# One layer of a hybrid decoder on one core: weight buffers of one width in two tiles, and weight sums made one step before their split

## The chip, the cores and the metric

The kernel runs on one core of a Trainium2 chip. Its engines work side by side, each through its own queue in order: PE (TensorE) multiplies matrices, DVE (VectorE) does elementwise arithmetic, ACT (ScalarE) copies and applies functions, POOL (GpSimd) and SP (SyncE) issue DMAs. The metric is the device time of one execution in microseconds (us). Before the change it was 2711.05 us, the median of 3 runs (2710.53 to 2716.68).

## The reference, cut to what matters

One layer with 512 positions and a model width of 2048, all in float32:

```python
mod = (silu(c) @ w_ada + b_ada)          # shifts, scales, gates
h = rms_norm(x, g_attn) * (1.0 + sc_a) + sh_a
x = x + gt_a * parallel_mixers(h, ...)   # sparse attention and latent attention, gated, then w_o
h = rms_norm(x, g_ffn) * (1.0 + sc_f) + sh_f
x = x + gt_f * conv_ffn(h, w_up, w_conv, b_conv, w_down)

def conv_ffn(h, w_up, w_conv, b_conv, w_down):
    u = h @ w_up                          # 512 x 2048 @ 2048 x 11264
    up = jnp.pad(u, ((0, 0), (CONV_W - 1, 0), (0, 0)))
    conv = b_conv
    for j in range(CONV_W):               # 3 taps over the positions, causal
        conv = conv + w_conv[j] * up[:, j:j + S]
    gate, val = jnp.split(conv, 2, axis=-1)
    return (jax.nn.silu(gate) * val) @ w_down   # 512 x 5632 @ 5632 x 2048
```

The change concerns the products with `w_up` and `w_down` and part of the mixers' gate projection.

## The kernel before

**Precision.** PE multiplies in a format narrower than float32. So every operand is split into a high part (a copy by ACT) and a low part (the rest, by DVE); helper `split`, lines 129 to 131. Each product is then three matmuls: high x high, high x low, low x high.

**Seven products.** Three loops use `seven` (line 935): a part of the gate projection (8 pairs), the up projection (40 of its 44 pairs), and the down projection (4 chunks of 5, 6, 6 and 5 row blocks, 8 pairs each). A "pair" is two column blocks of 128 of the weight. Its product, split into 2 x 2 blocks, is made with seven block products instead of eight. The weight comes as four blocks, `L[11]`, `L[21]`, `L[22]`, `L[12]`, each 128 partitions by K x 128 columns (1024 in the up projection, 640 or 768 in the down projection). The seven products need these blocks and sums of them: s3 = L21 - L11, then L21 + L22, that less L11, and L12 less the latter. DVE makes the sums, in place but for s3 (`comb`, line 979). The activations' sums are made beforehand.

**Steps.** A pair has seven steps, in the order p1, p7, p6, p2, p5, p4, p3. The function of that name (lines 995 to 1033) loads, sums and splits a step's weight; `prepare` (line 1065) calls it AHEAD steps before PE's matmuls of that step (2, and 3 in the down projection). A step has 3 K matmuls of 256 columns: 24 in the up projection, 15 or 18 in the down projection. After them `e1` to `e3` take the bank (a PSUM accumulator) out: a copy by ACT (lines 985 and 987) or a sum on DVE (lines 991 and 993), which I call bank sum. Two steps later, or one on another bank between, PE accumulates on the same bank again and must wait for that. After a pair's last step `ffn_out` convolves the two results (ACT line 1379, DVE lines 1380 and 1381), multiplies them and stores them as `f`; the down projection ends in a multiplication by the gate and a sum into `x1_d` or the output.

**Buffers.** Weights lie in raw buffers (`rawq`, a queue: a load takes the oldest, `done` puts one back at the end) and in buffers for the split (`hi_b`, `lo_b`, used in turn by the counter `cnt["wt"]`). `weight_bufs` makes them in a pool of their own: 5 raw of 1104 columns and 3 pairs for the split, and from the down projection on 7 raw of 768 and 4 pairs, for which the pool is closed and opened anew in the same memory (`turn`, line 1572, after the matmuls of the up projection's last step). There are also 81 slots of 512 columns for everything else (`get`, `put`); a slot that was put back rests for a few steps. In the first 34 of the 40 up pairs (`slots=True`) s3 and L12 don't lie in raw buffers but in two slots each; loads, sums and splits of them are then made in two pieces.

**Order.** Dependencies follow the stretches of a tile that instructions read and write. A planner orders each engine's instructions: it plays the program with its own estimates of durations and puts an instruction in its engine's queue when it believes that engine and data are ready, program order breaking ties. Weight loads go through SP's queue (line 968), which stands at a load until its buffer is free. POOL's queue stores and reloads f tiles (lines 1397, 1406 and 1482); `ahead` (line 1496) loads and splits these for the down projection as slots come free, from the last 56 steps of the up projection on.

## Time and profile before

| | us |
|---|---|
| median of 3 runs | 2711.05 |
| profiled execution | 2708.11 |
| its span, first to last instruction | 2706.3 |
| seven products of the gates, from the first matmul to the last | 614.5 to 784.7 |
| of the up projection, 34 pairs with slots | 1402.7 to 2100.7 |
| of the up projection, 6 pairs in raw buffers | 2100.7 to 2221.2 |
| of the down projection | 2227.1 to 2701.9 |

The profile is of one execution. Busy time is the time in which an engine ran an instruction; idle time before a group of instructions is put down to what ended it, the releaser. "DVE slot L981 <- DMA raw<-in_w_ups" reads: DVE, about to run line 981 with a slot as result, waited for a DMA from the up weights into a raw buffer. Where a column of numbers follows it, it is the total in us, the number of times and the longest. A line is often that of a helper: L130 and L131 are the high and the low part of every split, L981 every weight sum, L1082 to L1084 the matmuls of every step of seven products. DMA-issuing instructions stand on SPq, the sequencer of SP.

### The profile page before, as it was taken

The page shows a single profiled execution, that of the slowest core. Times are in us where ns is not written, and L with a number is a line of the kernel's source. Part 1 is how long each engine was busy: PE and PEld are TensorE (multiplying, and loading weights), DVE is VectorE, ACT ScalarE, POOL GpSimd, SP SyncE. Part 2 cuts the span into 40 slices and gives each one's busy share as a digit, 9 for nine tenths or more (in the row PEclk, how much of TensorE's full clock was granted, in tenths as well). Part 3 has the DMA queues.
Part 4 walks back from the last instruction along what each step waited for, and adds up shares of the span by engine and source line. Part 5 has one row for each costly group of instructions (what it writes and reads, how often), then busy time and mean ns, then how long its engine had stood idle before and what let it go on. Part 6 is the DMA issues. An engine that isn't in the chain of part 4 may idle for free.

```text
span 2706.3 us, 45437 instructions
## 1 busy us (share of the span) xinstructions
PE 2613.8 (97%) x17200; PEld 2345.9 (87%) x17200; DVE 2180.2 (81%) x3669; ACT 1281.9 (47%) x2069; POOL 363.6 (13%) x663
## 2 busy tenths in 40 slices
PE   6999999999999999999999999999999999999999
PEld 5787687778997767788789999999999988899999
DVE  7977976688878667983778888888889888778777
ACT  4333434334444455322545555555555555545454
POOL 1001011110032222110100000000001032413120
PEclk8999899999999999999999999999999999999999
DMA  9953136665585588962333343334334456767563
GB/s 340 339 160 98 33 112 213 196 217 164 195 265 158 164 260 283 332 231 94 133 128 114 124 139 115 127 114 141 127 110 148 131 178 181 188 163 192 138 204 116
DMA packets 220559, 464.33 MB, mean 172 GB/s; under 512 B 24330, under 2 KB 65700, under 8 KB 220340
## 3 DMA queue, kind: packets, MB, share of 16 engines
q1 hardware_dynamic: 175156, 344.93, 39.0%
q0 software_dynamic: 45152, 116.50, 15.0%
q8 instruction: 134, 2.20, 0.3%
q14 instruction: 85, 0.70, 0.1%
q10 hardware_dynamic: 32, 0.01, 0.0%
HBM read 397.11 MB, written 64.23 MB: 170 GB/s over the span
## 4 chain that ended last, share of the span: by engine, by line
PE 53%; DVE 16%; issue 15%; DMA 13%; POOL 2%; ACT 1%; SPq 0%; DVEq 0%; POOLq 0%; ACTq 0%
PE bank L134 9%; PE bank L135 9%; PE bank L136 9%; PE bank L1082 7%; PE bank L1083 7%; PE bank L1084 7%; DVE wlo L131 6%; DMA raw<-in_w_ups 5%; DMA slot<-in_w_ada 2%; DMA raw<-in_w_down 2%; DVE raw L981 2%; DVE slot L981 1%; DVE slot L1380 1%; DMA raw<-in_w_in 1%; DVE slot L1381 1%
## 5 line engine op out<-in xcount | busy, mean ns | idle before, releaser
L1082 PE MATMUL bank<-slot,whi 128*128 128x256 f32 x3920 | 1108.2, 283 | 44.8 <-DVE slot L991 13.1
L1083 PE MATMUL bank<-slot,whi 128*128 128x256 f32 x3920 | 1101.6, 282 | 0.4 <-DVE slot L131 0.4
L1084 PE MATMUL bank<-slot,wlo 128*128 128x256 f32 x3920 | 1094.3, 282 | 5.7 <-DVE wlo L131 5.6
L1082 PEld LDWEIGHTS bank<-slot,whi 128*128 128x128 f32 x3920 | 743.2, 190 | 58.3 <-DVE slot L993 16.5
L1084 PEld LDWEIGHTS bank<-slot,wlo 128*128 128x128 f32 x3920 | 737.2, 189 | 8.6 <-DVE wlo L131 8.3
L1083 PEld LDWEIGHTS bank<-slot,whi 128*128 128x128 f32 x3920 | 742.2, 189 | 0.9 <-DVE slot L131 0.6
L130 ACT ACTIVATE whi<-raw 128x1024 fp32r<-128x1024 f32 (+2 forms) x458 | 424.6, 928 | 463.8 <-PE bank L1083 352.0
L131 DVE TENSOR_TENSOR wlo<-raw,whi 128x1024 fp32r<-128x1024 f32 (+2 forms) x458 | 482.1, 1058 | 54.3 <-ACT whi L130 53.0
L122 ACT ACTIVATE whi<-raw 128x1024 fp32r<-128x1024 f32 (+4 forms) x182 | 187.2, 1031 | 392.0 <-PE bank L136 198.9
L123 DVE TENSOR_TENSOR wlo<-raw,whi 128x1024 fp32r<-128x1024 f32 (+4 forms) x182 | 216.5, 1191 | 147.7 <-ACT whi L122 146.3
L981 DVE TENSOR_TENSOR raw<-raw,raw 128x1024 f32<-128x1024 f32 (+2 forms) x252 | 265.2, 1053 | 68.7 <-DMA raw<-in_w_down 47.5
L135 PE MATMUL bank<-wlo,slot 128*128 128x512 f32 (+2 forms) x768 | 297.0, 387 | 0.9 <-DVE wlo L123 0.9
L134 PE MATMUL bank<-whi,slot 128*128 128x512 f32 (+2 forms) x768 | 289.6, 390 | 6.8 <-ACT slot L401 4.3
L136 PE MATMUL bank<-whi,slot 128*128 128x512 f32 (+2 forms) x768 | 292.0, 384 | 0.0
L135 PE MATMUL bank<-slot,whi 128*128 128x512 f32 (+1 forms) x656 | 263.0, 401 | 1.2 <-DVE slot L703 1.1
L134 PE MATMUL bank<-slot,whi 128*128 128x512 f32 (+1 forms) x656 | 260.8, 403 | 3.1 <-ACT slot L1370 2.3
L136 PE MATMUL bank<-slot,wlo 128*128 128x512 f32 (+1 forms) x656 | 257.5, 401 | 0.4 <-DVE wlo L123 0.4
L134 PEld LDWEIGHTS bank<-whi,slot 128*128 128x128 f32 x768 | 145.8, 190 | 38.1 <-ACT slot L401 4.4
L135 PEld LDWEIGHTS bank<-wlo,slot 128*128 128x128 f32 x768 | 146.2, 190 | 29.4 <-DVE wlo L123 1.4
L739 DVE SCALAR_TENSOR_TENSOR slot<-slot,c_act,slot 128x512 f32<-128x512 f32 x203 | 149.6, 749 | 25.3 <-DMA slot<-in_w_ada 24.3
L136 PEld LDWEIGHTS bank<-whi,slot 128*128 128x128 f32 x768 | 144.7, 189 | 28.4 <-issue 0.3
L130 ACT ACTIVATE whi<-slot 128x512 fp32r<-128x512 f32 x204 | 128.0, 628 | 82.0 <-PE bank L1083 60.7
(294 smaller groups left out, 3115.0 us busy)
## 6 DMA issues: line engine op xcount, KB each, us to landing
slot<-in_w_ada SPq DMA_DIRECT2D x344, 256.0 KB, 5.6
raw<-in_w_ups SPq DMA_DIRECT2D x126, 512.0 KB, 4.3
raw<-in_w_in SPq DMA_DIRECT2D x50, 512.0 KB, 3.6
raw<-in_w_down SPq DMA_DIRECT2D x64, 384.0 KB, 5.1
raw<-in_w_down SPq DMA_DIRECT2D x64, 320.0 KB, 4.2
slot<-f POOLq DMA_DIRECT2D x154, 128.0 KB, 3.8
slot<-in_w_ups SPq DMA_DIRECT2D x68, 256.0 KB, 2.7
f<-slot POOLq DMA_DIRECT2D x66, 256.0 KB, 5.3
```

What stands on the lines that cost most here:

```text
L122: A.activation(hi, raw[:, :w], AF.Copy)
L123: V.tensor_tensor(lo, raw[:, :w], r32(hi), ALU.subtract)
L130: A.activation(dst_hi, src, AF.Copy)
L131: V.tensor_tensor(dst_lo, src, r32(dst_hi), ALU.subtract)
L134: PE.matmul(o, lh, rh, start=first, stop=False)
L135: PE.matmul(o, lh, rl, start=False, stop=False)
L136: PE.matmul(o, ll, rh, start=False, stop=last)
L739: V.scalar_tensor_tensor(acc, ts[i], c_act[:, k:k + 1], acc, op0=ALU.mult, op1=ALU.add)
L981: V.tensor_tensor(part(o, x, y), part(a, x, y), part(b, x, y), op)
L1082: PE.matmul(o, wh[:, ks], rh, start=first and k == 0, stop=False, skip_group_check=True)
L1083: PE.matmul(o, wh[:, ks], rl, start=False, stop=False, skip_group_check=True)
L1084: PE.matmul(o, wl[:, ks], rh, start=False, stop=last, skip_group_check=True)
```

## The change

Five things are changed together.

1. All pairs of the up projection use raw buffers for s3 and L12, none uses slots; all loads, sums and splits are of one piece.
2. The raw buffers are stretches of one tile, `raw`, and those for the split stretches of another, `whl`; both exist for the whole program. `weight_bufs` lays them out anew without closing a pool. New raw buffers are put in the queue in the order in which the old ones at their place were put back.
3. A step has two functions: one that loads and sums (a1, a7, a6, a4), called one step before the other, which splits (p1 to p3). So s3, both sums of p6 and the sum into L12 (out of p5, into a4) are made one step before their split in program order. s3 takes the buffer that was put back last (`rawq.pop()`).
4. `turn` is called at every step of the up projection. At its last step but one it lays out the buffers anew, and at its last two steps it prepares the down projection's first two; a third is prepared after the loop.
5. The counter of the split buffers is set before the up projection so that its last three steps use them in the order 0, 1, 2.

```diff
-    wpool = ExitStack()
-    hi_b, lo_b, rawq = [], [], deque()
+    WR, WS = 5 * 1104, 6 * 1104
+    wraw = pool.tile([P, WR], F32, name="raw")
+    whl = pool.tile([P, WS], F32R, name="whl")
+    hi_b, lo_b, rawq, raw_at = [], [], deque(), []
+    cnt = {"wt": 0, "half": 0, "at": 0}
     def weight_bufs(nr, nh, w):
-        wpool.close()
-        wp = wpool.enter_context(tc.tile_pool(name=f"w{w}", bufs=1))
+        assert nr * w <= WR and 2 * nh * w <= WS and len(rawq) == len(raw_at)
+        age = [[i for i, t in enumerate(rawq) if t is b[0]][0] for b in raw_at]
+        def freed(x):
+            return max([a for a, (_, lo, hi) in zip(age, raw_at) if lo < x + w and x < hi], default=0)
+        raw_at[:] = [(wraw[:, i * w:(i + 1) * w], i * w, (i + 1) * w) for i in sorted(range(nr), key=lambda i: freed(i * w))]
         rawq.clear()
-        rawq.extend([wp.tile([P, w], F32, name=f"raw{w}_{i}") for i in range(nr)])
-        hi_b[:] = [wp.tile([P, w], F32R, name=f"whi{w}_{i}") for i in range(nh)]
-        lo_b[:] = [wp.tile([P, w], F32R, name=f"wlo{w}_{i}") for i in range(nh)]
+        rawq.extend(b[0] for b in raw_at)
+        hi_b[:] = [whl[:, 2 * i * w:(2 * i + 1) * w] for i in range(nh)]
+        lo_b[:] = [whl[:, (2 * i + 1) * w:(2 * i + 2) * w] for i in range(nh)]
+        cnt["wt"] = 0
...
-            def new(slots=False):
-                if slots:
-                    return [(get(), 0, T), (get(), T, W)]
-                return [(rawq.popleft(), 0, W)]
...
-            def load(blk, slots=False):
-                t = new(slots)
-                for b, x, y in t:
-                    SP.dma_start(b[:, :y - x], p.load(blk)[:, x:y])
+            def load(blk):
+                t = rawq.popleft()
+                SP.dma_start(t[:, :W], p.load(blk))
                 return t
...
             def comb(o, a, b, op):
-                for x, y in cuts(o, a, b):
-                    V.tensor_tensor(part(o, x, y), part(a, x, y), part(b, x, y), op)
+                V.tensor_tensor(o[:, :W], a[:, :W], b[:, :W], op)
...
-            def p1():
+            def a1():
                 L[11] = load(0)
                 L[21] = load(1)
+            def p1():
                 return hilo(L[11])
+            def a7():
+                L["s3"] = rawq.pop()
+                comb(L["s3"], L[21], L[11], ALU.subtract)
+                L[22] = load(3)
             def p7():
-                s3 = new(p.slots)
-                comb(s3, L[21], L[11], ALU.subtract)
-                r = hilo(s3)
-                done(s3)
-                L[22] = load(3)
+                r = hilo(L["s3"])
+                done(L["s3"])
                 return r
-            def p6():
+            def a6():
                 comb(L[21], L[21], L[22], ALU.add)
                 comb(L[11], L[21], L[11], ALU.subtract)
-                r = hilo(L[11])
-                L[12] = load(2, p.slots)
-                return r
+                L[12] = load(2)
+            def p6():
+                return hilo(L[11])
...
             def p5():
                 r = hilo(L[21])
+                done(L[21])
+                return r
+            def a4():
                 comb(L[12], L[12], L[11], ALU.subtract)
                 done(L[11])
-                done(L[21])
-                return r
...
+            return (((a1, p1), X, r11, e1, True), ((a7, p7), Y, t3, e7, True), ((a6, p6), X, t2, e6, False),
+                    ((none, p2), Z, r21, e2, False), ((none, p5), X, t1, e5, False),
+                    ((a4, p4), Y, t4, e4, False), ((none, p3), X, r22, e3, False))
         def prepare(q):
+            for i in range(0 if q == 0 else q + 1, min(q + 2, len(steps))):
+                steps[i][0][0]()
             if q < len(steps):
-                ready[q] = steps[q][0]()
-        def start():
-            for q in range(AHEAD):
+                ready[q] = steps[q][0][1]()
+        def start(*qs):
+            for q in qs or range(AHEAD):
                 prepare(q)
         def run(then=None):
             for q, (_, o, r, ev, first, K) in enumerate(steps):
                 prepare(q + AHEAD)
+                if then:
+                    then(q - len(steps))
...
-                if then and q == len(steps) - 1:
-                    then()
...
-    work = [Pair(rs, lambda blk, i=i: w_ups[i, blk], ffn_out(i), slots=i < NF_ - 10) for i in range(NF_ - 4)]
+    work_up = [Pair(rs, lambda blk, i=i: w_ups[i, blk], ffn_out(i)) for i in range(NF_ - 4)]
...
-    def turn():
-        weight_bufs(7, 4, 768)
-        down_start()
+    def turn(q):
+        if q == -2:
+            assert cnt["wt"] % 3 == 0
+            weight_bufs(7, 4, 768)
+        if q >= -2:
+            down_start(q + 2)
+    cnt["wt"] = 3 - len(work_up) * 7 % 3
     up_start()
     up_run(turn)
+    down_start(2)
     down_run()
```

26 lines of the change are left out of this document (7 added, 19 removed).

## The prediction

> **What bounds the kernel now.** I read the page first, then PE's waits, then a table of stages, then the instructions in order of time. In the first part of the page PE is busy for 97% of the span; the count of splits at L122 and the landing time of a weight load, below it, are used further down.
>
> ```profile
> span 2706.3 us, 45437 instructions
> ...
> PE 2613.8 (97%) x17200; PEld 2345.9 (87%) x17200; DVE 2180.2 (81%) x3669; ACT 1281.9 (47%) x2069; POOL 363.6 (13%) x663
> ...
> L122 ACT ACTIVATE whi<-raw 128x1024 fp32r<-128x1024 f32 (+4 forms) x182 | 187.2, 1031 | 392.0 <-PE bank L136 198.9
> ...
> raw<-in_w_ups SPq DMA_DIRECT2D x126, 512.0 KB, 4.3
> ```
>
> PE's waits (engine, line, releaser: us, times, longest) name DVE's bank sums (L993 in the up projection, L991 in the down projection):
>
> ```profile
> PE bank L1082 <- DVE slot L991: 13.1, 9, 3.1
> PE bank L1082 <- DVE slot L993: 11.2, 24, 1.2
> ```
>
> The table of stages (us; busy time of PE, PEld, DVE, ACT and POOL with their instructions; granted clock; DMA share; GB/s): the 34 pairs of the up projection with slots, its 6 pairs in wide buffers, the idle time at the turn, the first pair of the down projection, and its chunks of row blocks.
>
> ```profile
> 1402.70:2100.70 698.00, 683.17 (x5713) 676.43 (x5712) 619.79 (x893) 372.34 (x578) 44.66 (x83) 1.00 0.38 127
> 2100.70:2221.20 120.50, 119.59 (x1011) 119.14 (x1009) 108.71 (x137) 68.48 (x97) 25.04 (x47) 1.00 0.47 147
> 2221.20:2227.10 5.90, 0.28 (x4) 0.07 (x2) 2.82 (x5) 1.99 (x4) 2.64 (x5) 0.76 0.84 264
> 2227.10:2245.90 18.80, 15.86 (x106) 14.54 (x107) 18.71 (x31) 12.15 (x21) 6.39 (x12) 0.89 0.72 234
> 2245.90:2345.40 99.50, 91.61 (x737) 89.52 (x736) 79.49 (x120) 56.30 (x97) 33.09 (x52) 0.98 0.70 184
> 2345.40:2473.80 128.40, 122.89 (x1010) 120.56 (x1009) 100.91 (x133) 68.99 (x110) 35.24 (x56) 1.00 0.67 172
> 2473.80:2601.90 128.10, 121.84 (x1010) 120.29 (x1009) 98.84 (x133) 64.86 (x104) 32.41 (x49) 1.00 0.66 175
> 2601.90:2702.00 100.10, 100.10 (x842) 99.75 (x840) 81.86 (x122) 50.71 (x85) 9.56 (x17) 1.00 0.44 138
> ```
>
> Time divided by matmuls gives each stage's pace. A pair has 7 x 24 = 168 matmuls, so the first row has 34 x 168 = 5712 (122.2 ns each), the second 1008 (119.5 ns). The last chunk, where PE is never idle, takes 100.1 / 840 = 119.2 ns. At these paces the up projection has 698.0 - 5712 x 0.1195 = 15 us to give. The down projection has 99.5 - 735 x 0.1192 = 11.9, then 128.4 - 1008 x 0.1192 = 8.2 and 7.9: together 28. The turn, with its first pair of 105 matmuls, has 5.9 + 18.8 - 12.5 = 12.2. So 55 us is about all that this change can reach.
>
> What makes the bank sums late are DVE's own waits (same columns):
>
> ```profile
> DVE slot L981 <- DMA raw<-in_w_ups: 57.3, 29, 4.2
> DVE raw L981 <- DMA raw<-in_w_down: 47.5, 26, 3.9
> ```
>
> L981 is a weight sum. The planner has put it in DVE's queue where it believed the weights to have landed; they hadn't, and all behind it stands. In order of time (start, length, engine, line; in brackets the idle time before it and what ended it):
>
> ```profile
> 2288.77 4.50 SPq L968 DMA_DIRECT2D raw<-in_w_down  x4
> 2292.09 0.83 DVE L131 TENSOR_TENSOR wlo<-raw,whi 128x640 fp32r<-128x640 f32 x1 [0.28 <-ACT whi L130]
> 2295.38 0.83 DVE L981 TENSOR_TENSOR raw<-raw,raw 128x640 f32<-128x640 f32 x1 [2.46 <-DMA raw<-in_w_down]
> 2296.12 0.48 DVE L991 SCALAR_TENSOR_TENSOR slot<-bank,mod,slot 128x256 f32<-128x256 f32 x1
> 2296.65 0.39 PE L1082 MATMUL bank<-slot,whi 128*128 128x256 f32 x1 [1.49 <-DVE slot L991]
> ```
>
> Four loads go out in 4.5 us, the sum waits 2.46 us for one of them, the bank sum comes behind it, and PE stands for 1.49 us on its bank.
>
> **Part 1, which buffer a sum and a load use.** Before, the up projection's first 34 pairs put the s3 sum and block 2 in slots, so nothing but the landing holds s3 back, and the planner makes it far ahead of its split. After, s3 takes the buffer freed last, that of the previous pair's block 2: its sum can't stand in DVE's queue ahead of that block's last split (p3). The price is a wait, on DVE itself, and behind it in the queue are the splits of p1 and p7 and the bank sums. The new buffers free the loads earlier: L21 loads where the sum of the new a4 was the last to read L11, L22 after the split of p5 (was p4), L12 after that of p4 (was p3): one step earlier each. In the six wide pairs of before:
>
> ```profile
> 2127.39 1.22 DVE L981 TENSOR_TENSOR raw<-raw,raw 128x1024 f32<-128x1024 f32 x1
> 2128.86 1.22 DVE L131 TENSOR_TENSOR wlo<-raw,whi 128x1024 fp32r<-128x1024 f32 x1
> 2132.43 1.23 DVE L981 TENSOR_TENSOR raw<-raw,raw 128x1024 f32<-128x1024 f32 x1 [0.32 <-DMA raw<-in_w_ups]
> 2133.90 1.22 DVE L131 TENSOR_TENSOR wlo<-raw,whi 128x1024 fp32r<-128x1024 f32 x1
> 2135.74 1.23 DVE L981 TENSOR_TENSOR raw<-raw,raw 128x1024 f32<-128x1024 f32 x1 [0.62 <-DMA raw<-in_w_ups]
> 2137.22 1.22 DVE L131 TENSOR_TENSOR wlo<-raw,whi 128x1024 fp32r<-128x1024 f32 x1
> 2138.47 1.23 DVE L981 TENSOR_TENSOR raw<-raw,raw 128x1024 f32<-128x1024 f32 x1
> 2139.95 1.22 DVE L131 TENSOR_TENSOR wlo<-raw,whi 128x1024 fp32r<-128x1024 f32 x1
> ```
>
> The sum at 2127.39 frees L11, the load into it lands just before 2132.43 where s3 waits for it. After, s3 comes no sooner than the end of the split at 2133.90 (p3), that is 2135.1: some 2.7 us after the landing. L22, freed by the split at 2128.86, leaves by about 2130.1 and lands by 2134.4 with the page's 4.3 us; the sum that needs it can't come before 2136.2. Both waits in brackets go. So I give the 34 pairs the wide pairs' pace: -15 us. The bounds are 0 and, at the busy time alone of the wide pairs (119.59 / 1008 = 118.6 ns), 698.0 - 5712 x 0.1186 = 20.
>
> In the down projection the seven buffers keep their number. Before, L22 and L12 of a pair wait for p5 of the pair before, and the next two loads for p4 and p3: the burst of four above. After, L22 waits for p7 alone, L12 for the sum of a4, and L11 and L21 of the pair after for p5 and p4: spread over four steps, and s3 again behind p3. The sums find their weights landed. I take off what PE's row names, L991's 13.1 us: -13; the bounds are 0 and the 28 us above. The value lies in the middle because POOL's reloads of f tiles and their splits, untouched, keep DVE busy in the first three chunks (79 to 101 us of 100 to 128) and not in the last, the one without loss.
>
> **Part 2, fewer and wider instructions.** Five operations a pair (three splits, two sums) go from two of 512 columns to one of 1024, and two loads of 256 KB to one of 512 KB. From DVE's groups in the 34 pairs (the third is of the convolution, for later):
>
> ```profile
> L131 DVE TENSOR_TENSOR wlo<-raw,whi 128x1024 fp32r<-128x1024 f32 x137 | 167.3, 1221 | 4.7 <-ACT whi L130 3.9 <-PE bank L1083 0.7
> L131 DVE TENSOR_TENSOR wlo<-slot,whi 128x512 fp32r<-128x512 f32 x202 | 138.3, 686 | 0.4 <-ACT whi L130 0.3
> ...
> L1380 DVE SCALAR_TENSOR_TENSOR slot<-slot,wcv,slot 128x511 f32<-128x511 f32 x67 | 50.0, 748 | 4.2 <-ACT slot L1379 4.2
> ```
>
> That is 2 x 686 - 1221 = 151 ns each by duration, 34 x 5 x 0.151 = 26 us of DVE at most. I cost it at nothing: it hides behind PE (683 of 698 us), and the wide pace contains it. What could be lost is grain: a bank sum may wait behind 1.22 us where it waited behind 0.69; the wide pace contains that too.
>
> **Part 3, the sums a step ahead.** No instruction is added. In SP's queue the loads of a pair keep their order (L11, L21, L22, L12), each one step earlier; in the last chunk POOL's two loads of x1 go with them, past one step of f loads, and their slots are held one step longer: nothing, since POOL is busy there for 9.56 us of 100; in the chunks before, with 32 to 35 us, each could wait behind an f load. The gates' loop (56 steps, 1344 matmuls) already runs in wide buffers: 0; if it fell to the pace of the slot pairs, 2.7 ns a matmul, +4.
>
> **Part 4, the start of the up projection.** The count of split buffers is set to 2. Of 182 (L122) + 56 (gates) = 238 splits before it, taking the three buffers in turn, the last used buffer 0, so p1 would naturally take 1; now p1 takes 2 and p7 takes 0, the one PE leaves last. p7's split then falls where that of p6 falls now:
>
> ```profile
> 1396.44 1.34 ACT L130 ACTIVATE whi<-slot 128x512 fp32r<-128x512 f32 x2 [3.79 <-PE bank L135]
> 1402.74 1.06 ACT L130 ACTIVATE whi<-raw 128x1024 fp32r<-128x1024 f32 x1 [0.41 <-PE bank L135]
> 1404.53 1.22 DVE L131 TENSOR_TENSOR wlo<-raw,whi 128x1024 fp32r<-128x1024 f32 x1
> ```
>
> It would end at 1405.7; PE needs its low part at the third matmul of its second step, 24 x 0.1195 = 2.9 after 1402.7. About 0; at worst one step, +2.9.
>
> **Part 5, the turn.** Before, the new buffers wait for everything that lay in the old pool, PE's reading included:
>
> ```profile
> 2221.19 0.29 PE L1084 MATMUL bank<-slot,wlo 128*128 128x256 f32 x1
> 2221.51 2.70 SPq L968 DMA_DIRECT2D raw<-in_w_down  x6
> 2226.31 0.74 ACT L130 ACTIVATE whi<-raw 128x640 fp32r<-128x640 f32 x1 [3.57 <-DMA raw<-in_w_down]
> 2227.10 0.58 PE L1082 MATMUL bank<-slot,whi 128*128 128x256 f32 x1 [5.62 <-ACT whi L130]
> ```
>
> After, raw and split buffers lie in tiles of their own, a load waits only for what lies at its place, and the first two steps of the down projection are prepared during the last two of the up projection. What is late next is DVE: in the first pair it is busy for 18.71 of 18.80 us. Its idle time in the gap, 5.9 - 2.82 = 3.1 us, is the least that comes back; 12.2 the most. Since f-tile splits in that stretch can be planned later, I take -6.
>
> PE's clock there: in 7 us from 2224 on it is granted at half.
>
> ```profile
> 2224.00:2231.00 7.00, 3.83 (x16) 3.54 (x17) 4.24 (x8) 3.25 (x5) 2.23 (x5) 0.52 0.90 311
> ```
>
> The Trainium skill, in "TensorE: Matmul & The Clock Gate", Part 1, says that PE falls to half rate after an idle window of about 3.4 us and needs as much busy time to return. By that rule a gap under 3.4 us would also save half of the 3.9 us that PE ran slowly here, so the turn would give -8 and the kernel 2675; the trace's gap of 5.9 us agrees with it, and no shorter gap at a turn is in this trace.
>
> **The sum.** The profiled execution took 2708.1 us for a span of 2706.3; the median of the runs, 2711.05, lies 2.9 above it. -15 - 13 - 6 = -34: 2674 against the profiled time, 2677 as a median. A difference of 0.3% (8 us) is about what can be told from no change.
>
> **The rivals.** *All of it comes back*: -20 - 28 - 12 = -60 would need DVE never late; with a tenth of that kept, 2711 - 54 = 2657. The last chunk speaks for it, the f-tile splits against it.
>
> *The waits only move*: loads still land after the planner's guess, s3 stands in DVE's queue as before, and only the turn comes back: 2705. The wide pairs still have 0.32 and 0.62 us of it; against it stands the 2.7 us of room.
>
> *Slower, by what stands ahead of p7's split*: s3 is now tied behind p3, and the two other sums of a pair are planned a step earlier, ahead of that split. In the wide pairs it ends at 2141.2. Its step on PE is the second of the fourth pair from the end: 2221.2 - (4 x 168 - 24) x 0.1195 = 2143.8, so 2.6 us of room. If the planner puts the four convolution instructions (0.748 us each) and one more split (1.22) ahead of it, it is 4.2 - 2.6 = 1.6 us late; 40 pairs make +64, and -34 with it +30: 2741. It decides from 34 / 40 = 0.85 us a pair. Against it: the two sums at 2135.74 and 2138.47 stand ahead of it already.
>
> **How the numbers follow.** My forecast has 0.55, the larger gain 0.17, waits that only move 0.11, slower 0.17. The first two are faster, as are 0.06 of the third's spread around 2703: 0.78 faster, 0.05 same, 0.17 slower. The likeliest case's own range is 2660 to 2695 (bounds of the three terms, not all at once). The range takes in the larger gain, the third case and the lesser half of the slower one: 2652 to 2720.
>
> **What would show it.** Right: DVE's waits for in_w_ups and in_w_down at the sums under 15 us together (112 with the raw sums), PE's rows for L993 and L991 under 8, the up projection's 40 pairs at 119.5 ns a matmul, loads of in_w_down before the last matmul of the up projection, a gap under 3 us. Wrong: PE waiting at L1084 for low parts (L131), sums waiting for DMA, or a gap that stays because DVE is full.

## The result, and the profile after

The changed kernel takes 2672.65 us (median of 4 runs, 2670.49 to 2677.15); beside it the kernel before took 2713.86 (2710.53 to 2719.03). The ratio is 0.9849, with a 95% interval of 0.9826 to 0.9872. Forecast were 2677 and a range of 2652 to 2720. The profiled execution took 2670.49 us.

The first part of the page after: PE's busy time fell by 8 us, the span by 37.6.

```profile
span 2668.7 us, 45031 instructions
...
PE 2605.9 (98%) x17200; PEld 2343.3 (88%) x17200; DVE 2178.0 (82%) x3499; ACT 1266.9 (47%) x1967; POOL 362.2 (14%) x663
...
L968 DVE TENSOR_TENSOR raw<-raw 128x1024 f32<-128x1024 f32 (+2 forms) x320 | 347.2, 1085 | 5.0 <-DMA raw<-in_w_ups 1.9
```

The last line is the group of all weight sums (L968 now, L981 before). DVE's waits for weights at the sums have all but gone: of 57.3 and 47.5 us in the two rows shown of before, and 16.6 in a third one (`DVE raw L981 <- DMA raw<-in_w_ups`), one row is left, and none for `in_w_down`. The split is now L138 and L139, the load L957, the matmuls are L1086 to L1088, the bank copies L972 and L974, the bank sums L978 and L980.

```profile
DVE raw L968 <- DMA raw<-in_w_ups: 1.9, 2, 1.2
```

PE's waits from the first matmul of the up projection on name no bank sum any more. What is left waits for ACT and for low parts:

```profile
PE bank L1086 <- ACT slot L972: 5.5, 9, 1.3
PE bank L1086 <- ACT whl L138: 5.3, 6, 1.6
PE bank L1086 <- ACT slot L974: 3.7, 3, 1.3
PE bank L1088 <- DVE whl L139: 2.7, 4, 1.0
```

The same stages as before in the table of stages (columns as there):

```profile
1403.60:2082.90 679.30, 677.16 (x5714) 676.75 (x5713) 618.12 (x727) 360.08 (x478) 44.75 (x83) 1.00 0.40 133
2082.90:2207.90 125.00, 120.34 (x1010) 119.53 (x1009) 111.67 (x139) 68.48 (x98) 23.71 (x45) 1.00 0.47 154
2207.90:2208.00 0.10, 0.10 (x4) 0.10 (x3) 0.10 (x1) 0.00 (x1) 0.10 (x1) 1.00 0.91 353
2208.00:2225.60 17.60, 13.32 (x107) 12.50 (x105) 17.60 (x31) 13.03 (x24) 10.05 (x20) 1.00 0.77 249
2225.60:2316.30 90.70, 88.66 (x735) 87.42 (x736) 79.40 (x119) 54.17 (x94) 28.63 (x45) 1.00 0.73 185
2316.30:2441.30 125.00, 122.01 (x1011) 120.29 (x1010) 103.56 (x136) 69.83 (x112) 39.47 (x63) 1.00 0.71 188
2441.30:2564.50 123.20, 121.39 (x1010) 119.96 (x1009) 99.51 (x134) 65.22 (x106) 31.99 (x49) 1.00 0.68 178
2564.50:2664.10 99.60, 99.60 (x842) 99.60 (x841) 82.47 (x122) 50.78 (x85) 10.59 (x19) 1.00 0.45 145
```

By the starts of the matmuls (the table of all kernels below has them), the 34 pairs became 18.8 us shorter, the last six pairs 4.6 longer, the turn with its first pair 7.0 shorter, the down projection behind it 17.3 shorter. In all that is 38.5 us less, and the stages ahead of the up projection took 0.9 more.

The reason can be seen in the order of time. In the kernel before, the four loads of the burst left from 2288.77 to 2292.94, and the next one only at 2304.03, 11 us later. At that place of the down projection SP's loads are now spread: the seven of the first row below leave from 2279.71 to 2296.90, never more than 5.6 us apart. On DVE sums (L968) and splits (L139) alternate with the bank sums (L978) without a wait for a DMA:

```profile
2279.71 17.52 SPq L957 DMA_DIRECT2D raw<-in_w_down  x7
...
2286.18 0.81 DVE L139 TENSOR_TENSOR whl<-raw,whl 128x640 fp32r<-128x640 f32 x1
2286.91 0.81 DVE L968 TENSOR_TENSOR raw<-raw 128x640 f32<-128x640 f32 x1
2287.65 0.47 DVE L978 SCALAR_TENSOR_TENSOR slot<-bank,mod,slot 128x256 f32<-128x256 f32 x1
2288.04 0.81 DVE L139 TENSOR_TENSOR whl<-raw,whl 128x640 fp32r<-128x640 f32 x1
```

At the turn six loads of the down projection leave before the last matmul of the up projection, the first of them 20 us before it, and PE goes on without a gap (0.12 us from start to start):

```profile
2187.93 14.60 SPq L957 DMA_DIRECT2D raw<-in_w_down  x6
...
2207.87 0.28 PE L1086 MATMUL bank<-slot,whl 128*128 128x256 f32 x1
2207.99 0.28 PE L1087 MATMUL bank<-slot,whl 128*128 128x256 f32 x1
2208.10 0.40 PE L1088 MATMUL bank<-slot,whl 128*128 128x256 f32 x2
```

### The profile page after: what moved, and what is told of

Same layout as the page of the kernel before. It is cut to its first block, busy times and chain, and to the rows that moved or that the text cites. A ratio compares the mean times of both kernels' runs of the same rounds, so it can differ in the third digit from the quotient of the medians.

```text
span 2668.7 us, 45031 instructions
## 1 busy us (share of the span) xinstructions
PE 2605.9 (98%) x17200; PEld 2343.3 (88%) x17200; DVE 2178.0 (82%) x3499; ACT 1266.9 (47%) x1967; POOL 362.2 (14%) x663
## 5 line engine op out<-in xcount | busy, mean ns | idle before, releaser
L1086 PE MATMUL bank<-slot,whl 128*128 128x256 f32 x3920 | 1103.0, 282 | 20.3 <-ACT slot L972 5.5
L1087 PE MATMUL bank<-slot,whl 128*128 128x256 f32 x3920 | 1098.7, 281 | 0.2 <-DVE slot L139 0.2
L1088 PE MATMUL bank<-slot,whl 128*128 128x256 f32 x3920 | 1086.5, 281 | 4.9 <-DVE whl L139 4.9
L138 ACT ACTIVATE whl<-raw 128x1024 fp32r<-128x1024 f32 (+2 forms) x560 | 532.7, 953 | 622.0 <-PE bank L1087 405.5
L1086 PEld LDWEIGHTS bank<-slot,whl 128*128 128x128 f32 x3920 | 738.2, 188 | 28.0 <-ACT slot L972 8.6
L1087 PEld LDWEIGHTS bank<-slot,whl 128*128 128x128 f32 x3920 | 739.5, 189 | 0.6 <-DVE slot L139 0.5
L1088 PEld LDWEIGHTS bank<-slot,whl 128*128 128x128 f32 x3920 | 732.0, 188 | 6.2 <-DVE whl L139 6.2
L139 DVE TENSOR_TENSOR whl<-raw,whl 128x1024 fp32r<-128x1024 f32 (+2 forms) x560 | 605.9, 1087 | 123.8 <-ACT whl L138 121.5
L130 ACT ACTIVATE whl<-raw 128x1024 fp32r<-128x1024 f32 (+4 forms) x182 | 187.6, 1032 | 393.6 <-PE bank L144 191.7
L968 DVE TENSOR_TENSOR raw<-raw 128x1024 f32<-128x1024 f32 (+2 forms) x320 | 347.2, 1085 | 5.0 <-DMA raw<-in_w_ups 1.9
L131 DVE TENSOR_TENSOR whl<-raw,whl 128x1024 fp32r<-128x1024 f32 (+4 forms) x182 | 215.7, 1186 | 154.5 <-ACT whl L130 154.4
L143 PE MATMUL bank<-whl,slot 128*128 128x512 f32 (+2 forms) x768 | 297.6, 388 | 0.9 <-DVE whl L131 0.9
L142 PE MATMUL bank<-whl,slot 128*128 128x512 f32 (+2 forms) x768 | 290.9, 391 | 5.2 <-ACT slot L409 3.6
L144 PE MATMUL bank<-whl,slot 128*128 128x512 f32 (+2 forms) x768 | 292.5, 385 | 0.0
L142 PE MATMUL bank<-slot,whl 128*128 128x512 f32 (+1 forms) x656 | 263.0, 406 | 3.6 <-ACT slot L1372 2.3
L143 PE MATMUL bank<-slot,whl 128*128 128x512 f32 (+1 forms) x656 | 262.8, 401 | 0.5 <-DVE slot L711 0.5
L144 PE MATMUL bank<-slot,whl 128*128 128x512 f32 (+1 forms) x656 | 257.6, 401 | 1.2 <-DVE whl L131 1.2
L142 PEld LDWEIGHTS bank<-whl,slot 128*128 128x128 f32 x768 | 146.0, 190 | 36.7 <-ACT slot L409 3.7
L143 PEld LDWEIGHTS bank<-whl,slot 128*128 128x128 f32 x768 | 146.3, 190 | 30.1 <-DVE whl L131 1.3
L144 PEld LDWEIGHTS bank<-whl,slot 128*128 128x128 f32 x768 | 144.7, 189 | 29.5 <-issue 0.7
```

Of the source, the lines that this page charges most:

```text
L130: A.activation(hi, raw[:, :w], AF.Copy)
L131: V.tensor_tensor(lo, raw[:, :w], r32(hi), ALU.subtract)
L138: A.activation(dst_hi, src, AF.Copy)
L139: V.tensor_tensor(dst_lo, src, r32(dst_hi), ALU.subtract)
L142: PE.matmul(o, lh, rh, start=first, stop=False)
L143: PE.matmul(o, lh, rl, start=False, stop=False)
```

## The experiments

Theory: the gain comes from what a weight sum finds when DVE reaches it. In the kernel before the planner puts s3 ahead of its weights' landing; the order of the buffers moves it behind. Rivals: the width of the sums does it, the two tiles with the early turn do it, or making the sums one step ahead. Each part was tried alone or taken back. The table has the stages of all kernels from the starts of their matmuls (us), with the median of the runs and the ratio to the kernel before, timed beside each.

| kernel | up, 34 pairs | 6 pairs | gap | first pair | chunk 1, rest | chunk 2 | chunk 3 | chunk 4 | median | ratio (95%) |
|---|---|---|---|---|---|---|---|---|---|---|
| before | 698.1 | 120.4 | 5.9 | 18.8 | 99.5 | 128.4 | 128.1 | 99.9 | 2713.86 | 1 |
| changed | 679.3 | 125.0 | 0.1 | 17.6 | 90.8 | 125.0 | 123.3 | 99.5 | 2672.65 | 0.9849 (0.9826 to 0.9872) |
| e2_order | 674.0 | 125.8 | 6.3 | 17.4 | 92.5 | 129.5 | 126.3 | 101.5 | 2681.24 | 0.9873 (0.9856 to 0.9890) |
| e1_wide | 677.3 | 120.4 | 4.9 | 19.6 | 105.2 | 130.1 | 127.2 | 101.0 | 2699.15 | 0.9936 (0.9912 to 0.9959) |
| e3_turn | 695.6 | 119.9 | 0.1 | 18.9 | 106.6 | 131.0 | 127.4 | 99.6 | 2717.32 | 1.0008 (0.9999 to 1.0017) |
| e8_turn_order | 679.0 | 126.9 | 0.1 | 17.2 | 96.7 | 129.6 | 123.5 | 100.9 | 2684.70 | 0.9879 (0.9864 to 0.9893) |
| e5_fifo | 682.5 | 119.9 | 0.1 | 17.9 | 110.9 | 127.5 | 123.9 | 102.9 | 2701.97 | 0.9941 (0.9925 to 0.9957) |
| e4_sums_in_step | 680.7 | 126.2 | 0.1 | 17.6 | 90.3 | 124.9 | 123.0 | 99.6 | 2676.23 | 0.9857 (0.9842 to 0.9872) |
| e6_turn_late | 680.0 | 125.1 | 0.1 | 17.6 | 90.7 | 125.0 | 123.1 | 99.5 | 2673.64 | 0.9836 (0.9821 to 0.9851) |
| e7_act_order | 681.1 | 121.5 | 0.1 | 17.4 | 92.9 | 126.6 | 126.3 | 99.5 | 2681.89 | 0.9873 (0.9848 to 0.9899) |
| e9_f_early | 688.0 | 127.9 | 0.1 | 17.7 | 91.3 | 125.1 | 123.3 | 99.3 | 2684.03 | 0.9883 (0.9855 to 0.9912) |
| e10_pitch | 683.8 | 125.7 | 0.1 | 17.5 | 90.6 | 125.2 | 123.4 | 99.7 | 2677.33 | 0.9859 (0.9836 to 0.9882) |
| e11_slots64 | 677.2 | 124.8 | 0.1 | 17.7 | 90.0 | 125.5 | 123.4 | 99.5 | 2669.51 | 0.9832 (0.9807 to 0.9857) |
| e12_split32 | 678.4 | 124.6 | 0.1 | 17.9 | 91.0 | 125.3 | 124.2 | 99.8 | 2668.30 | 0.9833 (0.9801 to 0.9864) |

Stages ahead of the up projection, which no edit touches before the layout of the buffers, moved too: the gates' products took 170 to 175 us and the part between them and the up projection 614 to 621, without a pattern. Differences of some 4 us in a median are read with that in mind; where a stage is at issue, the stages are compared, not the medians.

### The tie alone, with nothing else changed (e2_order)

The kernel before, in which DVE's queue must hold the s3 sum behind the low part of the previous pair's p3. Slots, buffers, pools and the turn stay as they were.

```diff
             def p7():
                 s3 = new(p.slots)
-                comb(s3, L[21], L[11], ALU.subtract)
+                with tc.issue_after(low["p3"].ins) if "p3" in low else nullcontext():
+                    comb(s3, L[21], L[11], ALU.subtract)
...
                 r = hilo(L[12])
+                low["p3"] = low["last"]
...
-                    split(hi[:, x:y], lo[:, x:y], part(t, x, y))
+                    low["last"] = split(hi[:, x:y], lo[:, x:y], part(t, x, y))
```

> The kernel before, in which only one thing is fixed: in DVE's queue the sum s3 stands behind the last low-part split (p3) of the pair before, in all three loops. Buffers, loads, slots, instructions and the turn stay. Theory: DVE's waits for in_w_ups at s3 fall from 57 us to under 15, PE's wait on the bank sums L993 in the up projection from 9 to under 3, the up projection loses 12 to 18 us, the down projection (waits for in_w_down from 47 to under 20) 8 to 13: 2682 to 2693. Rivals A and B: neither the instructions nor the loads change, so no gain; if s3 was worth making early, slower, 2720 or more.

Its two rows of DVE's waits for weights (L983 is the sum here), and the 34 pairs in the table of stages:

```profile
DVE raw L983 <- DMA raw<-in_w_down: 22.5, 14, 3.1
DVE raw L983 <- DMA raw<-in_w_ups: 6.6, 4, 2.4
```

```profile
1403.70:2077.70 674.00, 674.00 (x5713) 673.95 (x5713) 627.18 (x892) 378.08 (x578) 44.77 (x83) 1.00 0.40 132
```

One instruction a pair held back gives 2714 - 2681 = 33 of the 41 us by the medians, and 25.8 of 38.5 us by the sums of the stages in the table. In the 34 pairs PE isn't idle at all, though sums and splits are still in two pieces and DVE does more work (627.18 us) than in the changed kernel (618.12). In the down projection a half of the waits is left, and chunks 2 and 3 are 1.1 us longer and 1.8 us shorter than before: there the tie alone isn't enough.

### Wide buffers alone (e1_wide)

The kernel before with s3 and L12 in raw buffers in all 40 pairs, so that their sums and splits are of one piece.

```diff
-    work = [Pair(rs, lambda blk, i=i: w_ups[i, blk], ffn_out(i), slots=i < NF_ - 10) for i in range(NF_ - 4)]
+    work = [Pair(rs, lambda blk, i=i: w_ups[i, blk], ffn_out(i)) for i in range(NF_ - 4)]
```

> The kernel before, with all 40 pairs of the up projection in raw buffers and nothing else changed. Theory (the sum s3 no longer stands in front of bank sums while its weights are in flight): the old order of buffers still lets s3 be planned early, but raw buffers come free later than slots, so the 34 pairs run at the pace of the six wide ones of before, 5712 x 0.1195 = 683 us instead of 698; DVE still waits some 1.2 us a pair for in_w_ups (7.3 us in six pairs). About 2698 against 2713, turn and down projection as before. Rival A (fewer, wider instructions are the gain): the same 683 us, with DVE's waits for the up weights as long as before, 60 us or more. Rival B (loads that leave a step earlier are the gain): no change, 2713.

DVE's waits for the up weights in the 34 pairs alone, a second row of before (beside the 57.3 us of the row for slots, all of which fall here) and then the only row of e1_wide; then e1_wide's row for the down weights and its 34 pairs in the table of stages:

```profile
DVE raw L981 <- DMA raw<-in_w_ups: 7.0, 16, 1.6
DVE raw L981 <- DMA raw<-in_w_ups: 47.9, 61, 2.2
...
DVE raw L981 <- DMA raw<-in_w_down: 52.2, 28, 4.4
```

```profile
1408.40:2085.70 677.30, 675.80 (x5713) 674.43 (x5712) 611.77 (x724) 365.30 (x477) 44.76 (x83) 1.00 0.40 132
```

The 34 pairs gain 20.8 us here too, although three quarters of DVE's waits are left: 47.9 of 64.3 us. It waits 61 times for at most 2.2 us in place of 45 times for up to 4.2, and PE is busy in 675.80 of 677.30 us, where it was idle for 14.8 us before. So the sum of DVE's waits doesn't say what they cost. The rows fit a simple reading, which no run tests by itself: a wait costs when it is longer than the lead of the splits and bank sums behind it. Nor do the runs tell whether the width does it or the raw buffers, which come free at other times than slots; e2_order, with narrow pieces in slots, shows that the width isn't needed. The down projection is as it was, or worse: the first chunk's rest took 105.2 us. So 20.8 us in one stage made 15 in the median, and 7.7 between the spans of the two profiled executions.

### The two tiles and the early turn alone (e3_turn), and with the tie (e8_turn_order)

e3_turn is the kernel before with the new `weight_bufs`, `turn` and counter, steps and slots as they were; e8_turn_order adds the tie of e2_order to it.

```diff
+    wraw = pool.tile([P, WR], F32, name="raw")
+    whl = pool.tile([P, WS], F32R, name="whl")
...
+    def turn(q):
+        if q == -2:
+            weight_bufs(7, 4, 768)
+        if q >= -2:
+            down_start(q + 2)
+    cnt["wt"] = 3 - len(work_up) * 7 % 3
```

> The kernel before with parts 2, 4 and 5 of the change alone: two tiles for raw and split buffers, laid out anew without closing a pool, the down projection's first two steps prepared during the last two of the up projection, the count of split buffers set. Slots, order of buffers and sums as before. Theory: the gap at the turn falls from 5.9 us to under 1, the first pair of the down projection from 18.8 to about 17, the rest of the down projection and the up projection stay as before: -6 to -8, 2705 to 2707. Rival (DVE is full there, the gap only moves): the first pair grows by what the gap loses, 2711 or more. Rival (the turn is worth all of its 12 us): 2701.

> The kernel before with two things: the new tiles and turn, and s3 tied behind the last split of the pair before in DVE's queue. Slots, old order of buffers and sums in the step of their split stay. Theory: the two add up once DVE has no waits in front of bank sums: 2681 with the order alone, less 6 for the turn, 2673 to 2677, with the down projection still 5 to 9 us above the changed kernel's chunks, since its loads still leave in bursts. Rival (the turn gives nothing whatever the order): 2681 to 2686.

The gap goes in both, and neither median is lower for it: e3_turn against the kernel before 1.0008 (0.9999 to 1.0017), e8_turn_order 2684.70 against 2681.24 for the tie alone. In e3_turn the first chunk gives it back, 106.6 us for 99.5. Its row in the table of stages has PE's clock at 0.95 and more idle time than before (11.5 us for 7.9), and the longest of PE's waits are bank sums (L999) that stand behind sums (L989):

```profile
2245.10:2351.70 106.60, 95.15 (x738) 92.48 (x737) 81.54 (x123) 57.25 (x99) 33.68 (x53) 0.95 0.66 174
```

```profile
PE bank L1092 <- DVE slot L999: 13.2, 11, 3.1
DVE raw L989 <- DMA raw<-in_w_down: 46.6, 28, 3.3
```

PE starts the down projection earlier and then meets the same late weights. With the tie it is otherwise. From the end of the up projection on, e8_turn_order takes 468.0 us and e2_order 473.5, so most of the 6.2 us of the gap is kept (some 1.7 of the 5.5 are a faster pace of PE with the new layout, the rest is the gap). It is the up projection that takes it back, 6.1 us longer than in e2_order. The time is that of the rival, but not for its reason. Of the 6.1 us, 2.3 are the pace of PE: matmuls that nothing delays (less than 135 ns from start to start) start 118.4 ns apart in its 34 pairs, 118.0 in e2_order; the section on where the buffers lie is about this. Another 2.0 us are two waits of PE in the first pair, which part 4 of the last account comes back to. The row of its 34 pairs, and DVE's waits:

```profile
1404.40:2083.40 679.00, 677.33 (x5713) 676.81 (x5712) 629.97 (x896) 378.42 (x580) 44.59 (x83) 1.00 0.39 131
```

```profile
DVE raw L991 <- DMA raw<-in_w_down: 29.3, 16, 3.0
```

So 29.3 us of the waits for the down weights are left with the tie, and none in the changed kernel. What the changed kernel has beyond e8_turn_order in the down projection, where there never were slots, is its order of buffers (and the sums a step ahead, which e4_sums_in_step below finds to be worth nothing): s3 takes the buffer freed last, and the loads take those freed earlier. Chunks 1 to 3 are 10.7 us shorter for it (349.8 to 339.1).

### s3 in the oldest buffer (e5_fifo)

The changed kernel; s3 takes its buffer at the other end of the queue.

```diff
-                L["s3"] = rawq.pop()
+                L["s3"] = rawq.popleft()
```

> The changed kernel in which s3 takes the buffer freed longest ago, as in the kernel before, instead of the one freed last. So s3 is no longer behind p3 of the pair before, and the loads of L22 and L12 come free one step later each. Theory: the planner again makes s3 early and the loads of the down projection leave in bursts; DVE waits for in_w_ups and in_w_down come back to 30 us or more each, the down projection's chunks lose 8 to 15 us, the up projection 0 to 5, as raw buffers alone held it at 677 us: 2682 to 2692. Rival (the step ahead or the width alone does it): within 4 us of the changed kernel, 2672 to 2677.

```profile
DVE raw L968 <- DMA raw<-in_w_ups: 56.6, 65, 3.6
DVE raw L968 <- DMA raw<-in_w_down: 50.8, 30, 4.3
```

One word brings the waits back, and 29 us with them by the medians, 25.0 by the stages: more than the 2682 to 2692 that were expected. The first chunk's rest is 20.1 us longer than in the changed kernel. In the up projection the waits are back as well, but the 34 pairs take only 3.2 us more, as in e1_wide: there the raw buffers alone keep PE fed. So in the up projection either part is enough, and in the down projection it is the place of s3. That place does two things: it holds s3 back, and it frees other buffers for the loads a step sooner. The second shows in SP's queue: over the rest of chunk 1 the longest pause between two loads is 11.1 us before, 9.9 in e8_turn_order and 12.3 here, and 6.0 in the changed kernel. Chunks 1 to 3 take 362.3 us here, 349.8 with the tie alone (e8_turn_order) and 339.1 in the changed kernel, so, if the two add up, each is worth about half there.

### Sums made in their own step (e4_sums_in_step)

The changed kernel with the sums of a step called just ahead of its split, as before.

```diff
-            for i in range(0 if q == 0 else q + 1, min(q + 2, len(steps))):
-                steps[i][0][0]()
             if q < len(steps):
+                steps[q][0][0]()
                 ready[q] = steps[q][0][1]()
```

> The changed kernel with its sums and loads called in the same step as the split that follows, not one step ahead; s3 still takes the buffer freed last. Theory: s3 is still tied behind the last split of the pair before, so DVE's waits for weights stay under 10 us and the time within 4 us of the changed kernel, 2672 to 2677. Rival (the step ahead is the gain): ACT waits for sums again, up and down projection lose half of what they won, 2685 to 2695.

No stage from the up projection on differs by over 1.4 us. The median is 3.6 us higher, within what untouched stages vary. DVE waits 9.4 us for `in_w_ups` in place of 1.9, 10 times, and PE doesn't feel it. The place in program order is worth nothing that can be measured here, which fits a planner that moves the sums as far as their buffers allow.

### The layout made only after the up projection (e6_turn_late)

```diff
-    up_run(turn)
-    down_start(2)
+    up_run()
+    weight_bufs(7, 4, 768)
+    down_start()
```

> The changed kernel with the turn put back: the buffers are laid out anew and the down projection's first three steps prepared only after the last step of the up projection. Theory: the gap comes back to 3 to 6 us, since the loads take that long although they need no longer wait for PE's reading; the first pair stays near 18; 2676 to 2682. Rival (the turn was worth nothing, as in the kernel before with the new turn alone): 2671 to 2675, the gap made good in the first chunk.

The gap is 0.12 us here too, and all stages are those of the changed kernel within 0.7 us: the time is the rival's, but neither text expected that the gap would stay closed. The early call isn't what closes it. With buffers in tiles that live on, a load depends only on what lies at its place, and the planner puts it ahead of the last matmuls by itself: the first load leaves at 2191.06, 20 us before the last matmul of the up projection, as in the changed kernel.

### The six last pairs: the scalar engine's order (e7_act_order, e9_f_early)

In the changed kernel the last six pairs take 125.0 us. Two breaks make it up, 42.7 us, or two pairs, apart. ACT at an ordinary end of a pair, and then at the second break (PE's rows last):

```profile
2105.66 1.06 ACT L138 ACTIVATE whl<-raw 128x1024 fp32r<-128x1024 f32 x1 [0.38 <-PE bank L1087]
2106.63 0.36 ACT L974 ACTIVATE slot<-bank 128x256 f32<-128x256 f32 x1
2108.49 1.07 ACT L138 ACTIVATE whl<-raw 128x1024 fp32r<-128x1024 f32 x1 [1.49 <-PE bank L1087]
...
2168.24 1.06 ACT L138 ACTIVATE whl<-raw 128x1024 fp32r<-128x1024 f32 x1 [0.38 <-PE bank L1087]
2171.06 1.06 ACT L138 ACTIVATE whl<-raw 128x1024 fp32r<-128x1024 f32 x1 [1.76 <-PE bank L1087]
2172.02 0.37 ACT L974 ACTIVATE slot<-bank 128x256 f32<-128x256 f32 x1
...
2172.44 0.39 PE L1086 MATMUL bank<-slot,whl 128*128 128x256 f32 x1 [1.30 <-ACT slot L974]
2179.42 0.39 PE L1086 MATMUL bank<-slot,whl 128*128 128x256 f32 x1 [1.03 <-ACT whl L138]
```

A bank copy (L974) that otherwise leaves right behind a split stands behind one split more, which waits 1.76 us for PE to be done with its buffer; PE then waits for the copy, and seven us later for a split. Two kernels look into it. e7_act_order forbids a split to pass the last bank copy made before it in program order; e9_f_early begins the f tiles' work at twice the distance.

```diff
-                split(hi, lo, t[:, :W])
+                with tc.issue_after(act["e"].ins) if "e" in act else nullcontext():
+                    split(hi, lo, t[:, :W])
...
-                    A.activation(o, b, AF.Copy, scale=g)
+                    act["e"] = A.activation(o, b, AF.Copy, scale=g)
...
-                    A.activation(o, b, AF.Copy)
+                    act["e"] = A.activation(o, b, AF.Copy)
```

> The changed kernel with one thing fixed in ACT's queue: a split stands behind the last copy out of a bank that the program has before it. In the changed kernel PE waits 9.4 us for such copies (5.5 for L972, 3.9 for L974), as the planner put a split that waits for PE's next step ahead of them. Theory: these waits fall under 2 us and the time by 4 to 9: 2664 to 2669. Rival (the copy itself waits for a slot, and now the splits stand behind it): no gain or slower, 2673 to 2685, PE waiting for high parts (L138) instead.

```diff
-        if q >= n - 56:
+        if q >= n - 112:
             ahead(q - n, 0)
```

> The changed kernel, with the f tiles of the down projection fetched again and split from 112 products before the end of the up projection on, not from 56. Theory (what the changed kernel still pays at the end of the up projection is a crowd on the scalar and vector engines: its last six pairs take 125.0 us where the 34 before them make 119.8 for six): the f work is spread over twice the pairs, the last six pairs fall to 120 to 122 us, the 34 before them stay at 678 to 681, time 2667 to 2671. Rival (the f work is put where the planner has room anyway, and tiles fetched early only hold their slots longer): last six pairs 124 to 127 us, time 2671 to 2676.

e7_act_order takes the breaks away (121.5 us) and pays more in the down projection: chunks 1 to 3 together are 6.7 us longer, and PE's waits for low parts grow from 2.7 to 7.2 us, probably because splits now stand behind copies that they needn't wait for. PE's waits for the copies are still 7.1 us in all, where under 2 were expected. Its median is 9 us above the changed kernel's, so it is no gain. e9_f_early missed both expectations: 2684.03, 11 us above. There is no crowd that can be spread: the same break, with the same lengths, now comes at the end of every second pair from 1971 us on, six times in place of two.

```profile
2013.87 0.38 PE L1086 MATMUL bank<-slot,whl 128*128 128x256 f32 x1 [1.30 <-ACT slot L974]
2020.86 0.38 PE L1086 MATMUL bank<-slot,whl 128*128 128x256 f32 x1 [1.03 <-ACT whl L138]
```

In each, two matmuls start 1.58 and 1.31 us after the one ahead, where 0.12 is usual: 2.65 us. Four more of them are 10.6 of the 11.6 us that the 40 pairs lost. So the break belongs to the planner's order in the stretch in which f tiles are fetched and split, not to how busy the engines are there: in this stretch ACT is busy for half of the time, and DVE for 85%, less than the 90% of all 34 pairs.

```profile
1970.00:2092.00 122.00, 115.11 (x960) 114.09 (x961) 103.73 (x120) 60.27 (x80) 6.46 (x12) 1.00 0.36 123
```

The breaks also need the tie. e2_order, with the buffers and the turn of before, has the same two (PE waits of 1.31 and 1.30 us for a copy, 42.6 us apart). In the table the six pairs take 119.9 to 120.4 us in the kernels that don't hold s3 back (before, e1_wide, e3_turn, e5_fifo) and 124.6 to 127.9 in all that do, but for e7_act_order. Why the planner lets the split pass the copy just there stays open.

### Where the buffers lie (e10_pitch, e11_slots64, e12_split32)

In these three only addresses move; instructions are those of the changed kernel. PE is all but never idle in the 34 pairs, and yet it is busy there for 674.0 us in e2_order and for 677.2 in the changed kernel.

```diff
-    WR, WS = 5 * 1104, 6 * 1104
+    WR, WS = 5 * 1120, 6 * 1120
...
-    weight_bufs(5, 3, 1104)
+    weight_bufs(5, 3, 1120)
```

> The changed kernel, with the five raw and six split buffers of the up projection at a pitch of 1120 columns (4480 bytes) in their two tiles, not 1104 (4416 bytes); nothing else is changed, and the widths read stay the same. Theory (the matmul's pace while it waits for nothing depends on where the split buffers lie: 0.1191 us in pairs that read buffer 1, 0.1181 to 0.1182 in the other two, and 0.1180 in the kernel before): all three buffers at 0.1180 to 0.1182, the 34 pairs at 676 to 678 us where they were 679.3, time 2668 to 2671. Rival (the pace goes with something else that falls on each third product, such as what the vector and scalar engines read and write meanwhile): one buffer in three stays at 0.1188 or more, the 34 pairs at 679 to 681, time 2671 to 2676.

```diff
-    rstd = pool.tile([P, 4], F32, name="rstd")
+    rstd = pool.tile([P, 16], F32, name="rstd")[:, 0:4]
```

> The changed kernel, with one small tile (rstd) widened from 4 to 16 columns, of which 4 are used, so that the 61 slots laid out behind it begin at a multiple of 64 bytes; they began 32 bytes past one. No instruction is added or removed. Theory (the matmul's pace depends on the place of its operands: in the trace of the changed kernel the undisturbed matmuls of the up projection that read a slot at a multiple of 64 start 117.9 ns after one another, those that read a slot 32 past one 118.6; in the down projection 117.8 and 118.7): all at about 117.9, so 0.7 ns for some 4,400 of the 5,712 matmuls of the 34 up pairs (679.3 us falls to 676) and 0.9 ns for some 2,800 of the down projection (-2.5 us), with the same in gates and earlier products -3 to -8 in all, time 2664 to 2670. Rival (the pace goes with the step of the product, not with the place of its operand): 34 pairs at 678.5 to 681, time 2671 to 2676.

```diff
-    WR, WS = 5 * 1104, 6 * 1104
+    WR, WS, OFF = 5 * 1104, 6 * 1104, 8
-    whl = pool.tile([P, WS], F32R, name="whl")
+    whl = pool.tile([P, WS + 2 * OFF], F32R, name="whl")
...
+        hi_b[:] = [whl[:, OFF + 2 * i * w:OFF + (2 * i + 1) * w] for i in range(nh)]
+        lo_b[:] = [whl[:, OFF + (2 * i + 1) * w:OFF + (2 * i + 2) * w] for i in range(nh)]
```

> The changed kernel, with the split buffers moved by 32 bytes in their tile, to the place within 128 bytes that they have in the kernel before (32 and 96 past a multiple of 128); the slots move by 64 bytes and so keep their place within 64. Theory (the place of the split buffers sets the pace): the kernel before's paces come back: 118.0 ns in the up projection instead of 118.4 (34 pairs at 675 to 677 us, was 679.3) and 119.0 to 119.2 in the down projection instead of 118.2 to 118.6 (chunks 2 and 3 0.5 to 1 us longer each), time 2668 to 2673. Rival (something else in the one-tile layout, such as all buffers in one tile, sets it): 34 pairs at 678.5 to 681, down projection as it is, time 2671 to 2676.

The row of the 34 pairs in each, in this order:

```profile
1405.10:2088.90 683.80, 681.48 (x5714) 680.87 (x5713) 618.02 (x726) 359.98 (x478) 44.75 (x83) 1.00 0.39 132
```

```profile
1403.20:2080.40 677.20, 675.06 (x5714) 674.60 (x5713) 618.01 (x727) 359.92 (x478) 44.65 (x83) 1.00 0.39 133
```

```profile
1400.80:2079.20 678.40, 676.13 (x5713) 675.50 (x5712) 617.86 (x727) 359.82 (x478) 44.66 (x83) 1.00 0.39 133
```

PE's busy time divided by 5712 matmuls is 118.0 ns in e2_order, 118.5 in the changed kernel, 119.3, 118.2 and 118.4 in these. The chip that a kernel ran on doesn't explain this. Counted from start to start of undisturbed matmuls, e4_sums_in_step, e6_turn_late and e9_f_early, which leave the layout alone and ran on three chips, have the changed kernel's 118.4 ns, and e10_pitch has 119.2 on the chip of e9_f_early. The pitch made every buffer slow where one in three had been: by the split buffer that a step reads, the changed kernel has 118.1, 118.2 and 118.9 ns, e10_pitch 119.2 for all three. Its theory of the place was right in kind and wrong in sign. Slots at multiples of 64 bytes gave 2.1 us of the 3.3 expected in the 34 pairs, and nothing in the down projection (chunk 2 125.5 for 125.0). The split buffers' place of before gave 0.9 of the 2 to 4 us expected and, as expected, a little back in the down projection (chunk 3 124.2 for 123.3). So where operands lie moves the pace of PE by up to 1% with nothing else changed; by which rule stays open, since every edit moved more than one kind of operand. The medians of e11_slots64 (2669.51) and e12_split32 (2668.30) are the lowest of all, but their intervals hold the changed kernel's ratio: no version here is shown to beat it.

## Why the prediction was right

The time came out 4 us below the forecast, and the terms stand in the profile close to their sizes: the up projection -14.2 (818.5 to 804.3) for -15, the turn with its first pair -7.0 for -6, the down projection -17.3 (455.9 to 438.6) for -13, all else +0.9 for 0.

The marks that it named are all there: 1.9 us of waits for weights at the sums, no row of PE for bank sums, 804.3 / 6720 = 119.7 ns a matmul over the 40 pairs, loads of `in_w_down` ahead of the last matmul, no gap. Two readings of before were of the wrong stretch: the row for L993 holds 1.9 us of the gates, so the up projection had 9.3 us of it, and DVE's waits with all raw sums were 121 us, not 112. Neither enters the sum. By its steps:

**The bound and its cause** (late bank sums behind sums that wait for DMA) was right. The tie alone gives two thirds of the gain by the stages and four fifths by the medians, and the queue's other end takes most of it back.

**Part 1, up projection.** The room in the six wide pairs was read rightly: the waits of 0.32 and 0.62 us went, with two of 1.2 at most left in all 40 pairs. But that -15 came out so close is luck, made of two errors. The 34 pairs took 118.9 ns a matmul, not the wide pairs' 119.5, which carried two waits of PE for bank sums (0.9 us in six pairs): -18.8, near the bound of 20. And the six pairs, whose pace was taken to stay, took 4.6 us more, by the breaks in ACT's order that come with the tie. That step, that the last six pairs cost what they did, failed; it priced no change of order on ACT. Besides, where the prediction put the gain of the 34 pairs down to the order of buffers, wide raw buffers with the old order gave it as well (e1_wide, -20.8).

**Part 1, down projection.** Taking off only what PE's row for L991 names was too little by 4 us. The row holds PE's waits for bank sums alone, while the first chunk also lost time to slowed matmuls (clock 0.98 before, 1.00 after) and late splits. There was a cap, as it said: chunks 1 to 3 stay 3 to 5 us each over the last chunk's pace of 119.2 ns. That the f tiles are the reason isn't shown; no run takes them away.

**Part 2** cost nothing, as forecast, but 26 us was too high a bound of what it saves DVE: busy time in the 34 pairs fell by 8.0 with wide buffers alone (619.79 to 611.77 in e1_wide). Durations of neighbours overlap: in the order of time before, the instruction behind a piece of 512 columns starts after 0.60 us though the piece lasts 0.69.

```profile
1514.46 0.69 DVE L981 TENSOR_TENSOR slot<-slot,raw 128x512 f32<-128x512 f32 x1
1515.06 1.22 DVE L131 TENSOR_TENSOR wlo<-raw,whi 128x1024 fp32r<-128x1024 f32 x1
1516.19 0.69 DVE L1463 TENSOR_TENSOR slot<-slot,slot 128x512 f32<-128x512 f32 x1
```

The piece of 1024 starts its successor after 1.13, so a pair of pieces costs 1.20 - 1.13 = 0.07 more, 12 us for 170 at most.

**Parts 3 and 4.** Nothing for the sums a step ahead: right (e4_sums_in_step). The up projection begins 0.9 us later, which is within what the stages ahead of it vary. But part 4 wasn't free. In the first pair PE waits twice, for a bank copy that stands behind a split and for a split:

```profile
1407.94 0.39 PE L1086 MATMUL bank<-slot,whl 128*128 128x256 f32 x1 [1.11 <-ACT slot L974]
1414.71 0.38 PE L1086 MATMUL bank<-slot,whl 128*128 128x256 f32 x1 [1.03 <-ACT whl L138]
```

These matmuls start 1.39 and 1.31 us after the one ahead, which makes 2.5 us, in place of "about 0" and inside the bound of 2.9. e3_turn and e8_turn_order have them at the same two matmuls of the first pair. Of the kernels without the new tiles and the counter, e1_wide and e2_order have no such wait in that pair, and the kernel before has one of 1.36 us at another place. Which of the two, tiles or counter, brings them isn't tested.

**Part 5.** The gap went and DVE was the next to be late, as named: in the first pair DVE is busy for 17.60 of 17.60 us. The rule of the Trainium skill ("TensorE: Matmul & The Clock Gate", Part 1) would have added the slow clock's time and made the turn -8. The trace agrees with its half about the clock: without an idle gap the rows at the turn have 1.00 where they had 0.76 and 0.89. A gap isn't the only thing that lowers it: e3_turn has none, and its first pair has 0.91. But that time came back only in part, since DVE bounds this pair: e2_order still has the gap and the clock at 0.86, and its first pair takes 17.4 us.

```profile
2203.50:2209.90 6.40, 0.43 (x5) 0.23 (x3) 3.42 (x6) 2.64 (x6) 2.48 (x5) 0.85 0.90 284
2209.90:2227.30 17.40, 15.89 (x105) 14.84 (x106) 17.40 (x29) 11.39 (x20) 6.40 (x12) 0.86 0.74 252
```

What the prediction didn't see is that this term doesn't stand alone. With the old order of sums it is worth nothing (e3_turn): a chunk that starts 6 us sooner meets its weights 6 us less ready. With s3 tied, most of it stays (e8_turn_order). Nor did it price what the new layout costs the up projection: 0.4 ns a matmul, 2.3 us in the 34 pairs. Of its two means, the early call is idle; the tiles do it (e6_turn_late).

**The rivals.** The slower one didn't happen: PE's waits for low parts are 2.7 us in four times from the up projection on, so p7's split was not late pair by pair; the rows shown of the down projection have sums and splits by turns, not sums gathered ahead of a split. That the waits only move is what e3_turn shows of the tiles, but not of the change.

## What to carry to other kernels

Where a planner with estimated durations orders an engine that takes its queue in turn, an instruction that depends on a DMA costs what stands behind it. A buffer chosen so that it can't be written early holds such an instruction back without an added instruction, and one line (which end of a queue) was worth 25 to 29 us here. Read a wait by its length against the lead of what is queued behind it, not by the total of its row: in the 34 pairs 47.9 us of DVE's waits, none over 2.2, go with 1.5 us of idle PE, and 64.3 us of them, up to 4.2 each, with 14.8. And a gain at a seam between stages is only kept if the next stage can use it; try it with the next stage's own limit removed and without, and compare the stages as well as the total, since another stage can hide it, as the up projection did in e8_turn_order.

## What the runs showed of the hardware

The pace of PE depends on where its operands lie, by up to 1%: with the same instructions, a granted clock of 1.00 and next to no idle time, 118.2 ns a matmul of 256 columns in e11_slots64 and 119.3 in e10_pitch. In the changed kernel one of the three split buffers is slower than the others (118.9 ns to 118.1 and 118.2); a pitch of 4480 bytes in place of 4416 made all of them slow. The Trainium skill, in "SBUF — State Buffer", section "Operand start alignment", tells which starts are allowed and says that its runs "timed nothing"; so the two can't be compared.
